# Attention scores from two matmuls in place of three: key parts stacked on the rows of the array

## The chip, the cores and the metric

The kernel runs on one core of a Trainium2 chip. The metric is the device time of one execution in microseconds (us), as the median of several runs. The profile is one execution, recorded by the hardware profiler; its times count from the start of its span.

## What is computed

The reference is a network of two layers on 512 latent tokens (x, width 1024) and 256 context tokens (ctx), in float32. Each layer normalises, projects to three head groups, mixes and projects back, then runs a gated feed-forward. The head groups are a long convolution (hyena), a gated mix over chunks of 128 tokens (sgu) and differential attention. Only the attention is touched by the change:

```python
def diff_attn_block(q, k, v, lam):
    s = jnp.einsum('bqhcd,bkhcd->bhcqk', q, k).astype(jnp.float32) * (DA_HEAD_DIM ** -0.5)
    a = jax.nn.softmax(s, axis=-1)
    w = a[:, :, 0] - lam * a[:, :, 1]
    return jnp.einsum('bhqk,bkhd->bqhd', w.astype(v.dtype), v)
...
        k_all = jnp.concatenate([k_c, k_l], axis=1)
        v_all = jnp.concatenate([v_c, v_l], axis=1)
        att_l = diff_attention(q_l, k_all, v_all, lam, subln_g[i], lam_init)
...
        if not last:
            att_c = diff_attention(q_c, k_c, v_c, lam, subln_g[i], lam_init)
```

There are 4 heads; each has two components c of 64 dimensions for q and k (both normalised and, for latents, rotated) and a value of 128. Latent queries see 512 + 256 keys in both layers; context queries see the 256 context keys, in the first layer alone.

## The kernel before

Every float32 operand of a matmul is kept as a high part and a low part in the type float32r: `split` (L230) writes hi = src on ScalarE and lo = src - hi on VectorE or POOL (GpSimd). A product is then three matmuls into one bank of PSUM, hi times hi, hi times lo and lo times hi: `mm3` (L245), lines L251, L252 and L253. Nearly all of TensorE's work goes through these three lines.

The tokens come in two streams, `lat` (512) and `con` (256). For each half j of the heads (two heads, h = 0 and 1), `kqv` (L616) projects k, q and v; `qk` (L538) takes the projected q or k per pair of token tiles, normalises, rotates, transposes each 128 x 128 block on TensorE (L593) and splits the result (L597). After the transpose the two components of a head lie on the rows: component 0 on rows 0 to 63, component 1 on rows 64 to 127. `kv_io` (L645) stores and loads the context's keys and values in DRAM. `attend` (L657) goes over query tiles qt of 128 and heads h; for each it computes the scores of both components c, three matmuls on 64 rows per source of keys (512 columns for latents, 256 for context), takes the maximum (L686) and the exponential (L691), combines the two components (L697), transposes the weights (L706) and multiplies with v (L718). For a latent query tile and a head that is twelve score matmuls: two components, each with three of 512 and three of 256 columns. The text calls this a unit.

The order of the work is set by Python generators: `woven` (L167) always advances the task with the smallest cost so far over its rate, where `self.cost` counts the time of matmuls as assumed by the program; `room` and `claim` hold a task back until the pools of buffers have space. UNITS (L127) gives the pools in units of 256 columns (1 KB on each partition): R for float32r operands, F for float32 work. The framework then orders each engine's instructions, so matmuls of other tasks stand between those of a unit in many places. Each engine runs its list in order. Weights are loaded by SP's queue; POOL's queue loads the tables of the convolution (L830) and the context's keys (L655).

The filter spectra of the convolution already use a product in two matmuls, the first on 128 rows, the second on 64:

```python
nc.tensor.matmul(flat(p.ap), lhsT=hid.hi[:, pos], rhs=w3[:, ch], start=True, stop=False)
nc.tensor.matmul(flat(p.ap), lhsT=hid.lo[half[0], pos], rhs=w3[half[0], ch], start=False, stop=True)
```

These are L905 and L906; L400 (16 short matmuls on 32 columns of the array for each weight tile) makes the modulation vectors.

Of the kernel before, what the change touches and what calls it, by code (L numbers as in the profile page):

```python
# [16 lines left out]
P = 128  # L17
# [11 lines left out]
HD = 64  # L29
# [3 lines left out]
CW = 256  # L33

TWO_PI = 2.0 * math.pi
SHARE = 4
# [89 lines left out]
BANKS = {"A": (0, 1, 6, 7), "H": (0, 1), "S": (2, 3, 4, 5), "W": (6, 7), "P": (6, 7)}  # L126
UNITS = {"R": 104, "RW": 24, "F": 44, "FW": 24}  # L127

# [21 lines left out]
class Net:  # L150
# [387 lines left out]
    def qk(self, st, l, c, i, rope):  # L538


        nc, nt, T = self.nc, st.nt, st.T
        w = self.win(st, l, c)
        outs = self.pairs(2, T)
        tab = self.rope[i]
# [44 lines left out]
        for t, _, sq in work:  # L589
            pt = self.ps("W", 2, 2, P)  # L590
            for h in range(2):
                for z in range(2):
                    nc.tensor.transpose(pt[:, h, z], sq[:, z, h * P:(h + 1) * P], self.ident)  # L593
            for h in range(2):
                src = pt[:, h].rearrange("p z q -> p (z q)")
                cols = slice(t * P, (t + 2) * P)
                self.split(src, *outs[h][:, cols])  # L597
            pt.free()
            sq.free()

    def vproj(self, st, l, c):
# [14 lines left out]
    def kqv(self, st, l, j, rope, q=True):  # L616

        n = st.T // 64
        st.held[j] = n * (3 if q else 2)
        yield from self.claim(st.held[j])  # L620
# [17 lines left out]
    def kv_load(self, st, j, mem):  # L638
        st.held[j] = 8
        yield from self.claim(8)  # L640
        st.k[j] = self.pairs(2, st.T)
        st.vv[j] = [Pair.one(self.r(2, 2, CW))]
        self.kv_io(st, j, mem, False)

    def kv_io(self, st, j, mem, store):  # L645

        off = 0
        for b in st.k[j] + st.vv[j]:
            sb = flat(b.whole.ap)
            dr = mem[:, j, off:off + sb.shape[1]]  # L650
            off += sb.shape[1]
            if store:
                self.nc.sync.dma_start(dr.bitcast(F32), sb.bitcast(F32))
            else:
                self.nc.gpsimd.dma_start(sb, dr)  # L655

    def attend(self, st, l, j, srcs):  # L657
# [9 lines left out]
        for qh in range(0, st.nt, 2):  # L667
# [3 lines left out]
            for h in range(2):  # L671
                q = st.q[j][h]
                ws = []
                for qt in (qh, qh + 1):
# [3 lines left out]
                    for c in range(2):  # L678
                        b = self.ps("S", nk)
                        r = slice(c * HD, (c + 1) * HD)  # L680
                        off = 0
                        for s in reversed(srcs):
                            self.mm3(b[:, off:off + s.T], [(q[r, qt * P:(qt + 1) * P], s.k[j][h][r, :])])
                            off += s.T
# [938 lines left out]
```

## Time and profile before

| | |
|---|---|
| median of 3 runs | 1915.76 us (1915.36 to 1921.28) |
| the profiled execution | 1918.05 us, span 1916.3 us |
| granted TensorE clock, mean | 0.963 |
| TensorE (PE) busy | 1797.2 us, 94% of the span |
| VectorE (DVE), ScalarE (ACT), GpSimd (POOL) busy | 1079.3, 676.9, 118.0 us |
| matmuls in the trace | 10938 |

PE's busy time is that of matmuls, which overlap in the records (each is shown until its end leaves the array); what a matmul costs is the step from its start to the next start. PEld are the loads of the stationary operand. A clock of 1.0 is 2.4 GHz, 0.5 is 1.2 GHz. L12 is line 12 of the kernel; for the three matmuls of `mm3` all products share the three lines, and the score matmuls are those with 64 rows.

### The profile page before, as it was taken

The numbers are of one execution on the slowest core, as the hardware profiler recorded it, in microseconds if no ns is written. First come the engines' busy times: TensorE is split into PE (matmuls) and PEld (weight loads), VectorE is DVE, ScalarE is ACT, GpSimd is POOL, SyncE is SP. The second block draws the span as 40 slices with busy tenths as digits, with TensorE's granted clock in tenths as the row PEclk, the third lists the DMA queues.
The fourth block names the chain that finished last, engine by engine and source line by source line (L and its number), as shares of the span: only waits on it lengthen the run. The fifth ranks groups of instructions, "written<-read, shape, count | busy, mean of one in ns | idle before, by whom it ended". The sixth has DMA issues, their size and how long they took to land.

```text
span 1916.3 us, 27513 instructions
## 1 busy us (share of the span) xinstructions
PE 1797.2 (94%) x10938; PEld 1532.3 (80%) x10938; DVE 1079.3 (56%) x2243; ACT 676.9 (35%) x1167; POOL 118.0 (6%) x127
## 2 busy tenths in 40 slices
PE   4799898888997999999999999899999999999999
PEld 1478798677776888888888888789988798888887
DVE  5677786876868533332323244779588773333333
ACT  2534434443535321212121222633455452222221
POOL 1100223311001000000000000011000000000000
PEclk9799899799997999999999999899999899999999
DMA  8667644335454434343424135453213222323321
GB/s 274 198 222 237 212 155 133 111 101 162 144 174 137 153 99 136 90 136 110 149 86 146 61 112 174 138 171 124 72 43 111 73 62 64 115 83 102 93 93 65
DMA packets 101819, 245.39 MB, mean 128 GB/s; under 512 B 9748, under 2 KB 21750, under 8 KB 101690
## 3 DMA queue, kind: packets, MB, share of 16 engines
q1 hardware_dynamic: 93450, 221.71, 36.3%
q0 software_dynamic: 8240, 21.92, 3.9%
q8 instruction: 86, 1.41, 0.3%
q14 instruction: 43, 0.35, 0.1%
HBM read 221.18 MB, written 22.41 MB: 127 GB/s over the span
## 4 chain that ended last, share of the span: by engine, by line
PE 72%; DVE 7%; ACT 2%; issue 1%; DMA 1%; POOL 0%; DVEq 0%; ACTq 0%
PE banks L251 23%; PE banks L252 22%; PE banks L253 22%; PE banks L706 1%; PE banks L400 1%; DVE tiny L686 1%; PE banks L279 1%; DMA F<-x_ctx 1%; DVE F L459 1%; DVE RW L233 0%; ACT F L506 0%; ACT F L691 0%; DVE F L1028 0%; DVE F L1189 0%; DVE F L1026 0%
## 5 line engine op out<-in xcount | busy, mean ns | idle before, releaser
L251 PE MATMUL banks<-R,RW 128*128 128x512 f32 (+1 forms) x1984 | 698.3, 353 | 8.1 <-ACT R L507 2.9
L252 PE MATMUL banks<-R,RW 128*128 128x512 f32 (+1 forms) x1984 | 695.2, 351 | 2.6 <-DVE R L510 2.6
L253 PE MATMUL banks<-R,RW 128*128 128x512 f32 (+1 forms) x1984 | 693.4, 350 | 1.7 <-DVE RW L233 1.7
L232 ACT ACTIVATE RW<-FW 128x1024 fp32r<-128x1024 f32 (+2 forms) x240 | 240.3, 1002 | 563.9 <-PE banks L252 427.5
L251 PEld LDWEIGHTS banks<-R,RW 128*128 128x128 f32 x1984 | 379.0, 191 | 66.8 <-issue 5.6
L252 PEld LDWEIGHTS banks<-R,RW 128*128 128x128 f32 x1984 | 378.8, 191 | 51.9 <-DVE R L510 3.9
L253 PEld LDWEIGHTS banks<-R,RW 128*128 128x128 f32 x1984 | 378.1, 191 | 50.1 <-DVE RW L233 2.1
L233 DVE TENSOR_TENSOR RW<-FW,RW 128x1024 fp32r<-128x1024 f32 (+2 forms) x228 | 263.1, 1154 | 243.5 <-ACT RW L232 225.7
L1189 DVE SCALAR_TENSOR_TENSOR F<-banks,mods,F 128x512 f32<-128x512 f32 (+1 forms) x192 | 116.3, 615 | 177.1 <-PE banks L253 150.6
L251 PE MATMUL banks<-R 128*128 128x256 f32 (+3 forms) x584 | 185.0, 336 | 30.7 <-ACT R L1039 12.3
L252 PE MATMUL banks<-RW,R 128*128 128x256 f32 x624 | 178.9, 287 | 2.3 <-DVE RW L233 2.2
L251 PE MATMUL banks<-RW,R 128*128 128x256 f32 x624 | 180.1, 289 | 0.8 <-ACT RW L232 0.7
L253 PE MATMUL banks<-RW,R 128*128 128x256 f32 x624 | 179.0, 287 | 0.0
L252 PE MATMUL banks<-R 128*128 128x256 f32 (+3 forms) x584 | 176.6, 316 | 0.0
L253 PE MATMUL banks<-R 128*128 128x256 f32 (+3 forms) x584 | 175.2, 312 | 1.3 <-DVE R L1041 1.3
L251 PEld LDWEIGHTS banks<-R 128*128 128x128 f32 (+1 forms) x584 | 114.8, 205 | 55.9 <-ACT R L1039 14.6
L1207 DVE TENSOR_TENSOR F<-F,banks 128x256 f32<-128x256 f32 (+1 forms) x71 | 40.0, 565 | 203.8 <-PE banks L253 189.9
L232 ACT ACTIVATE R<-F 128x512 fp32r<-128x512 f32 (+1 forms) x133 | 71.8, 550 | 222.9 <-DVE F L1207 159.8
L252 PEld LDWEIGHTS banks<-R 128*128 128x128 f32 (+1 forms) x584 | 117.5, 205 | 8.8 <-issue 3.0
L252 PEld LDWEIGHTS banks<-RW,R 128*128 128x128 f32 x624 | 120.8, 194 | 4.6 <-DVE RW L233 3.7
L251 PEld LDWEIGHTS banks<-RW,R 128*128 128x128 f32 x624 | 120.8, 194 | 3.7 <-issue 1.0
L253 PEld LDWEIGHTS banks<-RW,R 128*128 128x128 f32 x624 | 120.9, 194 | 0.7 <-issue 0.2
(158 smaller groups left out, 1681.1 us busy)
## 6 DMA issues: line engine op xcount, KB each, us to landing
FW<-in_ffn_w SPq DMA_DIRECT2D x104, 512.0 KB, 3.7
FW<-in_ada_w SPq DMA_DIRECT2D x96, 512.0 KB, 5.3
FW<-in_w_in_tm SPq DMA_DIRECT2D x50, 512.0 KB, 4.7
R<-in_tab POOLq DMA_DIRECT2D x28, 512.0 KB, 5.9
FW<-in_w_in_cm SPq DMA_DIRECT2D x24, 512.0 KB, 4.7
F<-x_ctx SPq DMA_DIRECT2D x36, 256.0 KB, 3.4
FW<-in_ffn_w SPq DMA_DIRECT2D x24, 384.0 KB, 3.1
x_ctx<-F SPq DMA_DIRECT2D x32, 256.0 KB, 2.4
```

The source lines that it names most:

```text
L232: self.nc.scalar.activation(hi, src, AF.Copy)
L233: (lo_eng or self.nc.vector).tensor_tensor(lo, src, hi.bitcast(F32), op=ALU.subtract)
L251: mm(out, lhsT=lh, rhs=rh, start=(i == 0), stop=False)
L252: mm(out, lhsT=lh, rhs=rl, start=False, stop=False)
L253: mm(out, lhsT=ll, rhs=rh, start=False, stop=(i == n - 1))
L279: nc.tensor.matmul(p1[:, t:t + 1], lhsT=sq[:, t * P:(t + 1) * P], rhs=self.ones[:, 0:1], start=True, stop=True)
L400: nc.tensor.matmul(pa[32 * j:32 * j + 32, :], lhsT=self.cv[:, k, :], rhs=ws[j // 2][:, j % 2, z], start=(k == 0), stop=(k == KT - 1), tile ...
L459: nc.vector.tensor_tensor(st.acc[:, cols], st.acc[:, cols], q.ap, op=ALU.add)
L686: nc.vector.tensor_reduce(m, b.ap, axis=AX.X, op=ALU.max)
L706: nc.tensor.transpose(p[:, i, z, :], ws[z][:, (a + i) * P:(a + i + 1) * P], self.ident)
L1189: self.nc.vector.scalar_tensor_tensor(x, p, self.mods[l][:, sec * 8 + k, st.v:st.v + 1], x, op0=ALU.mult, op1=ALU.add)
L1207: nc.vector.tensor_tensor(s.ap, s.ap, u, op=ALU.mult)
```

## The change

Keys: for each head the buffer has two slots of T columns, one for each component c. In slot c the high part lies on the component's own 64 rows and the low part on the other 64 rows. Queries: three slots; slot c has the high part on its own rows and, copied by a DMA on POOL's queue, again on the other rows; slot 2 has the low parts of both components, each on its own rows. A score is then one matmul on 128 rows (high part of q, doubled, times high and low part of k: two products in one) and one on 64 rows (low part of q times high part of k). The three products are the same as before. Each transposed block of 128 rows is split in two halves of 64 rows, since they go to different slots. Pool R has 108 units in place of 104, F has 40 in place of 44, and the cost given to the weaver for a score is two thirds of the old one.

```diff
+ROWS = [slice(0, HD), slice(HD, P)]
-UNITS = {"R": 104, "RW": 24, "F": 44, "FW": 24}
+UNITS = {"R": 108, "RW": 24, "F": 40, "FW": 24}
...
-        outs = self.pairs(2, T)
+        outs = [self.r(3 - i, T) for _ in range(2)]
...
             for h in range(2):
-                src = pt[:, h].rearrange("p z q -> p (z q)")
                 cols = slice(t * P, (t + 2) * P)
-                self.split(src, *outs[h][:, cols])
+                for z, own in enumerate(ROWS):
+                    src = pt[own, h].rearrange("p z q -> p (z q)")
+                    self.split(src, outs[h][own, z, cols], outs[h][ROWS[1 - z], z, cols] if i else outs[h][own, 2, cols])
             pt.free()
             sq.free()
+        if i == 0:
+            for h in range(2):
+                for z, own in enumerate(ROWS):
+                    nc.gpsimd.dma_start(outs[h][ROWS[1 - z], z], outs[h][own, z])
...
-        st.held[j] = n * (3 if q else 2)
+        st.held[j] = n * (7 if q else 4) // 2
...
-                        r = slice(c * HD, (c + 1) * HD)
+                        r, tq = ROWS[c], slice(qt * P, (qt + 1) * P)
                         off = 0
                         for s in reversed(srcs):
-                            self.mm3(b[:, off:off + s.T], [(q[r, qt * P:(qt + 1) * P], s.k[j][h][r, :])])
+                            k, out = s.k[j][h], b[:, off:off + s.T]
+                            nc.tensor.matmul(out, lhsT=q[:, c, tq], rhs=k[:, c], start=True, stop=False)
+                            nc.tensor.matmul(out, lhsT=q[r, 2, tq], rhs=k[r, c], start=False, stop=True)
+                            self.cost += s.T / 1200
                             off += s.T
```

In the changed program the two score matmuls are L692 (128 rows) and L693 (64 rows), the copies of q are L607, and other lines move down by 1 to 11 (L593 is L596, L706 is L717, L251 to L253 are L252 to L254, L830 is L841, L655 is L663).

The order on TensorE near the end of the latents' attention in the second layer (score matmuls read R alone). Before, one unit:

```order
L251 MATMUL banks<-R 128x512
L252 MATMUL banks<-R 128x512
L253 MATMUL banks<-R 128x512
L251 MATMUL banks<-R 128x256
L252 MATMUL banks<-R 128x256
L253 MATMUL banks<-R 128x256
L251 MATMUL banks<-R 128x512
L252 MATMUL banks<-R 128x512
L253 MATMUL banks<-R 128x512
L251 MATMUL banks<-R 128x256
L252 MATMUL banks<-R 128x256
L253 MATMUL banks<-R 128x256
```

Now:

```order
L692 MATMUL banks<-R 128x512
L693 MATMUL banks<-R 128x512
L692 MATMUL banks<-R 128x256
L693 MATMUL banks<-R 128x256
L692 MATMUL banks<-R 128x512
L693 MATMUL banks<-R 128x512
L692 MATMUL banks<-R 128x256
L693 MATMUL banks<-R 128x256
L717 MATMUL banks<-ident_100,F 128x128 x6
```

A unit has eight matmuls in place of twelve, and 128 and 64 rows alternate from each to the next, where all twelve had 64 rows.

The order on TensorE where the context's attention begins (L593 and L596 are the last transposes of q, L400 and L401 the modulation). Before:

```order
L593 MATMUL banks<-ident_100,F 128x128 x4
L400 MATMUL banks<-FW,cv_82 32x256 x4
L251 MATMUL banks<-R 128x256
L252 MATMUL banks<-R 128x256
L251 MATMUL banks<-R 128x256
L252 MATMUL banks<-R 128x256
```

Now:

```order
L596 MATMUL banks<-ident_100,F 128x128 x4
L401 MATMUL banks<-FW,cv_82 32x256 x16
L378 MATMUL banks<-ident_100,F 128x128 x2
L252 MATMUL banks<-R,RW 128x512
L253 MATMUL banks<-R,RW 128x512
L254 MATMUL banks<-R,RW 128x512
L692 MATMUL banks<-R 128x256
L693 MATMUL banks<-R 128x256
```

More of other work stands between the transposes and the first score, and the scores stand in pairs.

The order on POOL before the latents' first attention (L830 and L841 load tables, L655 and L663 the context's keys and values). Before:

```order
L830 DMA R<-in_tab 128x256 x6
L655 DMA R<-kv_73 128x512
L830 DMA R<-in_tab 128x256 x2
L655 DMA R<-kv_73 128x512
L655 DMA R<-kv_73 128x1024
L1025 TENSOR_TENSOR F<-F 128x256 x2
```

Now:

```order
L841 DMA R<-in_tab 128x256 x2
L607 DMA R<-R 64x512
L841 DMA R<-in_tab 128x256 x2
L663 DMA R<-kv_73 128x1024
L607 DMA R<-R 64x512 x3
L1036 TENSOR_TENSOR F<-F 128x256 x2
```

The four copies of q stand among loads that wait for buffers of the same pool.

## Rows read from the trace of the kernel before

**Rows 1.** The page, busy time of each engine in us (share of the span) and instructions.

```profile
PE 1797.2 (94%) x10938; PEld 1532.3 (80%) x10938; DVE 1079.3 (56%) x2243; ACT 676.9 (35%) x1167; POOL 118.0 (6%) x127
```

**Rows 2.** The stretches with score matmuls: length, busy us of each engine, clock, DMA.

```profile
125.00:215.00 90.00, 83.49 (x601) 66.76 (x600) 65.97 (x181) 40.77 (x86) 10.37 (x14) 0.96 0.72 234
345.00:435.00 90.00, 77.69 (x471) 64.18 (x472) 67.00 (x157) 44.09 (x88) 17.02 (x14) 0.86 0.35 106
...
500.00:585.00 85.00, 82.11 (x532) 61.33 (x532) 62.84 (x145) 41.84 (x84) 0.58 (x1) 1.00 0.50 163
...
1365.00:1435.00 70.00, 69.89 (x476) 61.19 (x475) 57.38 (x145) 36.41 (x68) 0.00 (x0) 0.98 0.12 37
...
1480.00:1545.00 65.00, 57.90 (x312) 50.06 (x312) 47.86 (x115) 33.71 (x64) 0.00 (x0) 0.84 0.21 65
```

**Rows 3.** Timeline, TensorE, feed-forward: start us, us, line, operands; first and last of ten.

```profile
1700.16 0.39 PE L251 MATMUL banks<-R,RW 128*128 128x512 f32 x1
...
1702.20 0.39 PE L251 MATMUL banks<-R,RW 128*128 128x512 f32 x1
```

**Rows 4.** Timeline, TensorE, a whole unit of the second layer.

```profile
1510.73 0.28 PE L252 MATMUL banks<-R,RW 128*128 128x256 f32 x1
1510.86 0.28 PE L253 MATMUL banks<-R,RW 128*128 128x256 f32 x1
1511.06 0.50 PE L251 MATMUL banks<-R 64*128 64x512 f32 x1
1511.40 0.39 PE L252 MATMUL banks<-R 64*128 64x512 f32 x1
1511.64 0.39 PE L253 MATMUL banks<-R 64*128 64x512 f32 x1
1511.64 0.50 PE L251 MATMUL banks<-R 64*128 64x512 f32 x2
...
1512.69 0.28 PE L253 MATMUL banks<-R 64*128 64x256 f32 x1
1512.90 0.33 PE L706 MATMUL banks<-ident,F 128*128 128x128 f32 x1
```

**Rows 5.** Groups by form, TensorE: the first matmul of each score triple.

```profile
L251 PE MATMUL banks<-R 64*128 64x512 f32 x64 | 33.0, 523 | 5.6 <-DVE F L798 2.8 <-ACT F L691 2.5
...
L251 PE MATMUL banks<-R 64*128 64x256 f32 x80 | 24.2, 316 | 1.6 <-DVE F L909 1.5
```

**Rows 6.** Timeline, TensorE, the filter spectra: 128 and 64 rows in turn.

```profile
185.60 0.50 PE L905 MATMUL banks<-R 128*128 128x512 f32 x1
186.03 0.50 PE L906 MATMUL banks<-R 64*128 64x512 f32 x1
186.46 0.50 PE L905 MATMUL banks<-R 128*128 128x512 f32 x1
186.90 0.50 PE L906 MATMUL banks<-R 64*128 64x512 f32 x1
```

**Rows 7.** Groups by form, VectorE and ScalarE: splits of 256 columns from PSUM.

```profile
L233 DVE TENSOR_TENSOR R<-banks,R 128x256 fp32r<-128x256 f32 x46 | 18.8, 417 | 1.4 <-ACT R L232 1.3
...
L232 ACT ACTIVATE R<-banks 128x256 fp32r<-128x256 f32 x46 | 17.2, 384 | 19.0 <-DVE R L233 11.7 <-PE banks L593 6.8 <-PE banks L984 0.5
```

**Rows 8.** DMA issues with KB and us to landing, and one issue on POOL's timeline.

```profile
kv<-R SPq DMA_DIRECT2D x8, 256.0 KB, 4.6
...
R<-in_tab POOLq DMA_DIRECT2D x14, 128.0 KB, 2.4
...
1444.37 0.53 POOL L655 DMA_DIRECT2D R<-kv  x1 [3.76 <-PE banks L253]
```

**Rows 9.** Timeline, TensorE, scores after a wait.

```profile
1515.74 0.79 PE L251 MATMUL banks<-R 64*128 64x512 f32 x1 [2.52 <-ACT F L691]
1516.33 0.62 PE L252 MATMUL banks<-R 64*128 64x512 f32 x1
```

**Rows 10.** The stretch around it, columns as in rows 2.

```profile
1514.00:1528.00 14.00, 12.03 (x46) 10.42 (x46) 11.07 (x33) 7.41 (x15) 0.00 (x0) 0.51 0.10 28
```

More of the change, by code (lines that the diff above doesn't have):

```diff
@@ L640, in kv_load @@
         yield from self.claim(8)
-        st.k[j] = self.pairs(2, st.T)
+        st.k[j] = [self.r(2, st.T) for _ in range(2)]
         st.vv[j] = [Pair.one(self.r(2, 2, CW))]
@@ L648, in kv_io @@
         for b in st.k[j] + st.vv[j]:
-            sb = flat(b.whole.ap)
+            sb = flat((b.whole if isinstance(b, Pair) else b).ap)
             dr = mem[:, j, off:off + sb.shape[1]]
```

## The prediction

> **What bounds the kernel now.** I read the page first: TensorE is busy 94% of the span, VectorE 56% and ScalarE 35%, so time is lost or won on TensorE unless a stretch waits [rows 1]. Then the table of stretches. The score matmuls stand in five stretches, together 400 us, and in these TensorE is busy 83.5 of 90, 77.7 of 90, 82.1 of 85, 69.9 of 70 and 57.9 of 65 us: it is idle for 28.9 us in all, and VectorE (some 300 us) follows well below it [rows 2]. So these stretches are bound by TensorE's order of work, with some waiting in the second and the last. "Busy" overstates the array, since matmuls overlap in the records; the rate is read from starts. Undisturbed 128-row matmuls of 512 columns start every 0.227 us (nine steps in 2.04 us) [rows 3], those of 256 columns every 0.12 us [rows 4].
>
> **What a score matmul costs now.** There are 144 triples, 64 with 512 columns and 80 with 256 [rows 5], all on 64 rows. In [rows 4] a whole unit of twelve (two components, each 3 x 512 and 3 x 256 columns) begins after a 128-row matmul. Three things are to be seen.
> - Streaming: 64-row matmuls step at 0.24 and 0.12 us, like those on 128 rows. Fewer rows buy nothing.
> - The change between 64 and 128 rows has a price on both sides. The last 256-column matmul ahead of it takes 0.20 us to the next start in place of 0.12, the first after it 0.34 in place of 0.23: 0.19 us for one change. Coming back, 1512.69 to 1512.90 is again 0.21 in place of 0.12.
> - The two components use different row halves, and they run partly side by side: a 512-column matmul of the second component starts at 1511.64 together with one of the first. The unit takes 1.84 us; its columns alone are 6 x 0.23 + 6 x 0.12 = 2.10, with the two edges 2.30. Side by side saves 0.46 us.
>
> **The pattern that the change makes stands already in the trace.** The filter spectra use a 128-row and a 64-row matmul in turn (L905, L906), the same shapes as the new pair. Their starts are 185.60, 186.03, 186.46 and 186.90: 0.43 us each where 0.227 would do [rows 6]. So one change of height costs 0.20 us, and in the new pairs every matmul has one on each side.
>
> **The change part by part.**
> 1. *Removed*: 144 matmuls, 64 x 0.23 + 80 x 0.12 = 24.3 us of TensorE.
> 2. *Changes of height*: in the order of the built programs I counted the places where the tile size of the array changes from one matmul to the next: 317 before, 425 now. The 64-row excursions rise from 103 to 160, because L692 and L693 alternate, while before six or twelve 64-row matmuls often stood together. 108 x 0.20 = +21.6 us.
> 3. *Side by side*: a 128-row matmul takes both halves, so nothing runs beside it. The old order has ten whole units of twelve and fifteen shorter runs with both halves; with half the saving for these, 10 x 0.46 + 15 x 0.23 = +8.0 us. Per unit: a whole one took 1.84 and some 0.2 outside it; the new eight are 4 x 0.23 + 4 x 0.12 + 8 x 0.20 = 3.0 us. A lone 256-column triple gains: 0.36 + 0.40 becomes 0.24 + 0.40. A rule of the Trainium skill (TensorEngine Tiling, Theoretical Speedup) gives up to twofold speed for operands of at most 64 rows; by it the old unit would take 1.05 us, this term would be some +21, and the sum 13 us higher. The trace shows 1.84, so the measured 0.46 stays.
>
>    TensorE together: -24.3 + 21.6 + 8.0 = +5.3 us. Little of it falls into idle time, which is 28.9 of 400 us [rows 2].
> 4. *Evictions of q and k*: each transposed block is now split in two row halves, 44 more ScalarE and 44 more VectorE instructions. Half the rows do not shorten an instruction whose columns stay, so 44 x 0.384 = 17 us and 44 x 0.417 = 18 us [rows 7]. Neither engine is the bound, and the projection matmuls of v and weights of other tasks hide them; uncovered they would cost up to 18 us, covered nothing. Nearest to cover: VectorE has about a quarter of these stretches free. I take +2.
> 5. *Copies of q*: 24 copies on POOL's queue, four for each of six q blocks, 128 KB for latents and 64 KB for context. Nothing before copies inside the chip's own memory. Nearest rows: a 128 KB load lands 2.4 us after issue, a 256 KB store from the same buffer in 4.6, and POOL holds 0.53 us to issue one [rows 8]. A score matmul thus follows its last q transpose by at least 0.38 (eviction) + 0.53 + 2.4 = 3.3 us, before about 1 us. The new order has over 20 us of other TensorE work there for the first heads' half of the latents (both layers), but only some 2.3 us for the context's first block (16 short ones, two transposes, three of 0.227 us) and 3.5 to 4 us for the other three (fifteen of 0.227 us in the last); ScalarE may also be late with the eviction. Four places at 1 us: +4; bounds 0 and 4 x 3.5 = 14, by the 4.6 us row.
>    On POOL the copies stand behind table and key loads that wait for buffers; the order shows them interleaved, and none of those loads waits for work that comes after the q transposes by more than 2 us of matmuls.
> 6. *Buffers and costs*: 4 units of 1 KB go from F to R, the weaver's costs fall by a third for scores. What is next to what changes in all queues; no row prices this. I put 0 with +-6.
>
> Sum: 5.3 + 2 + 4 = +11.3 us. The profiled execution took 1918.05 us, so it would be 1929; the median of the runs shown is 2.3 us lower, 1915.76, which gives **1927.0 us**.
>
> **The rivals.**
> - *Faster.* The changes of height cost less in the new pairs, or fall into waiting. Then -24.3 + 8.0 + 4 = -12 us, 1904. It decides at a price of (24.3 - 8.0 - 6) / 108 = 0.095 us per change. For it: the second stretch idles 12 us. Against it: [rows 6] has the very pattern, at twice that price. The Trainium skill (TensorEngine Tiling, Key Properties) says that a change of tiling mode, unlike a change of tile, drains the array; by that rule this rival falls, and the trace agrees in both: 0.20 us for the change, none between the two halves in [rows 4]. Chance 0.17.
> - *No difference.* The extra 5.3 us of TensorE and the copies' waits fall into idle time that is there anyway, 28.9 us, or the shuffled order gives back some: 1918. For it: TensorE's surplus is a difference of large terms. Chance 0.23.
> - *Much slower.* The copies are late: POOL, in order, waits for a table's buffer, all work behind the first score matmul stands still for 3.5 us at four places (+10 over the forecast), and TensorE's clock falls once more as it does now around 1515.74: there the engine had waited 2.52 us, and a first score matmul takes 0.59 us to the next start in place of 0.34 [rows 9]; in the 14 us around it the granted clock is 0.51, the lower level (1.2 GHz), and 12.0 us of busy time at half speed are 6 us lost [rows 10]. 1927 + 10 + 6 = 1943. It decides when copies land more than 4 us after the transposes. Chance 0.12.
> - The forecast itself, slower by 6 to 20 us: 0.48.
>
> **Numbers.** A measurement of this kernel tells about 0.3% (5.7 us) from no change. Slower is 0.48 + 0.12 = 0.60, within 0.23, faster 0.17. The range goes from half the removed price hidden (-8 us, 1908) to most of the late-copy case (+26, 1942).
>
> **What would show it.** In the new profile L692 and L693 of 512 columns should start 0.43 us apart, those of 256 columns 0.32; a whole unit should take 3.0 us. Copies should land in 2 to 5 us, and before the first L692 of an attention TensorE should wait about 1 us in four places. The page's TensorE count falls by 144. Wrong would be: pairs at 0.23 + 0.23, which is the first rival; or TensorE idle for several us on a copy, which is the third. If both are as foretold and the time still falls, it is the order of the other work that changed.

## The result and the profile after

The change is slower: 1984.88 us (median of 4 runs, 1980.69 to 1988.03) against 1915.79 us, a ratio of 1.0352 with a 95% interval of 1.0325 to 1.038, or +69 us. The forecast was 1927.0 us in a range of 1908 to 1942: right in its direction, wrong in its size, and above even the rival "much slower". The profiled execution took 1988.03 us, its span 1986.1 us at a mean clock of 0.943 (0.963 before).

The page, the row that answers to [rows 1]:

```profile
PE 1843.3 (93%) x10794; PEld 1542.5 (78%) x10794; DVE 1103.1 (56%) x2287; ACT 692.7 (35%) x1209; POOL 131.2 (7%) x151
```

144 matmuls are gone, VectorE has 44 and ScalarE 42 instructions more (44 each were foretold), POOL the 24 copies. But TensorE's busy time rose by 46 us.

TensorE's timeline of the kernel after, a whole undisturbed unit (start us, us, line, operands), against [rows 4]:

```profile
555.99 0.48 PE L692 MATMUL banks<-R 128*128 128x512 f32 x1
556.39 0.50 PE L693 MATMUL banks<-R 64*128 64x512 f32 x1
556.82 0.38 PE L692 MATMUL banks<-R 128*128 128x256 f32 x1
557.14 0.38 PE L693 MATMUL banks<-R 64*128 64x256 f32 x1
557.45 0.49 PE L692 MATMUL banks<-R 128*128 128x512 f32 x1
557.87 0.50 PE L693 MATMUL banks<-R 64*128 64x512 f32 x1
558.30 0.38 PE L692 MATMUL banks<-R 128*128 128x256 f32 x1
558.61 0.38 PE L693 MATMUL banks<-R 64*128 64x256 f32 x1
558.92 0.44 PE L717 MATMUL banks<-ident,F 128*128 128x128 f32 x2
```

The pairs step at 0.43 us (512 columns) and 0.32 us (256), the unit takes 2.93 us: the prices foretold (0.43, 0.32, 3.0).

So most of the time is elsewhere. Stretches with score matmuls, aligned between the two kernels by the same transposes and ends (length; busy us and instructions of PE, PEld, DVE, ACT, POOL; clock; DMA share; GB/s). First the kernel after:

```profile
125.00:225.00 100.00, 87.47 (x551) 64.48 (x550) 63.31 (x169) 38.55 (x80) 14.21 (x21) 0.87 0.64 203
345.00:440.00 95.00, 79.56 (x388) 61.96 (x386) 58.94 (x144) 38.33 (x79) 22.09 (x20) 0.71 0.30 89
505.00:560.00 55.00, 45.52 (x242) 36.49 (x241) 38.23 (x98) 24.91 (x53) 2.10 (x4) 0.84 0.45 125
1390.00:1440.00 50.00, 49.79 (x343) 45.10 (x343) 32.44 (x80) 25.82 (x50) 2.11 (x4) 1.00 0.32 90
1500.00:1545.00 45.00, 42.89 (x217) 31.55 (x218) 35.91 (x89) 22.08 (x44) 2.58 (x5) 1.00 0.41 124
```

The same stretches of the kernel before:

```profile
125.00:208.00 83.00, 78.78 (x580) 63.05 (x579) 59.59 (x164) 37.18 (x77) 8.35 (x12) 0.98 0.70 227
320.00:406.00 86.00, 70.89 (x454) 59.15 (x453) 64.48 (x157) 40.52 (x83) 19.93 (x18) 0.88 0.32 97
475.00:514.00 39.00, 36.21 (x250) 30.95 (x249) 34.04 (x92) 21.98 (x46) 0.63 (x1) 1.00 0.51 163
1334.00:1384.00 50.00, 49.82 (x353) 45.96 (x352) 28.79 (x73) 23.41 (x43) 0.00 (x0) 1.00 0.25 79
1442.00:1475.00 33.00, 32.95 (x198) 26.32 (x196) 29.07 (x71) 18.65 (x37) 0.53 (x1) 1.00 0.40 131
```

The five are 17, 9, 16, 0 and 12 us longer. They don't hold quite the same work: outside the scores the second has 38 matmuls fewer than before and the fifth 35 more, some 7.5 us of its 12, so these lengths are rough. In the third (223 and 224 other matmuls) and the fourth (328 and 327) the work is the same. Where the copies had over 20 us of other TensorE work ahead and the work is the same (the fourth), nothing is lost; the second stretch also had that cover, and its scores wait for no copy, so its loss has another cause. In the first three TensorE is idle for 12.5, 15.4 and 9.5 us (before 4.2, 15.1 and 2.8) and its clock is lower. By the page, 2 x (1 - clock) x span, the time at the lower level, is 226 us, 142 before.

TensorE's timeline of the kernel after, the start of the third attention block:

```profile
539.52 0.39 PE L254 MATMUL banks<-R,RW 128*128 128x512 f32 x1
543.54 0.50 PE L692 MATMUL banks<-R 128*128 128x512 f32 x1 [3.63 <-DMA R<-R]
543.97 0.79 PE L693 MATMUL banks<-R 64*128 64x512 f32 x1
544.70 0.58 PE L692 MATMUL banks<-R 128*128 128x256 f32 x1
...
553.04 0.63 PE L254 MATMUL banks<-R,RW 128*128 128x512 f32 x1
553.47 0.63 PE L252 MATMUL banks<-R,RW 128*128 128x512 f32 x1
553.89 0.53 PE L253 MATMUL banks<-R,RW 128*128 128x512 f32 x1
554.26 0.39 PE L254 MATMUL banks<-R,RW 128*128 128x512 f32 x1
```

TensorE waits 3.63 us for a copy of q. It is the longest of the waits that the profile puts down to the copies (us in all, times, longest):

```profile
PE banks L692 <- DMA R<-R: 6.3, 3, 3.6
```

A further wait of 2.09 us, ahead of the score that starts at 197.13, ends where a copy lands (197.00), though the profile names another releaser. The copies are thus waited for some 8 us in all. Right after the longest wait the pair steps at 0.73 us and ordinary matmuls at 0.43 us, until 553.9. The table of stretches has that piece, columns as above:

```profile
543.60:553.90 10.30, 10.30 (x22) 6.47 (x23) 4.17 (x8) 2.17 (x4) 0.00 (x0) 0.52 0.34 66
```

A clock of 0.52 (the level of 1.2 GHz) for 10.3 us of full work costs another 5 us: a late copy is paid more than once.

The copies wait for something themselves. POOL's timeline of the kernel after, the four copies of that block:

```profile
536.95 0.55 POOL L607 DMA_DIRECT2D R<-R  x1 [32.67 <-ACT R L233]
538.78 0.53 POOL L607 DMA_DIRECT2D R<-R  x1 [1.28 <-ACT R L233]
539.98 0.51 POOL L607 DMA_DIRECT2D R<-R  x1 [0.67 <-ACT R L233]
541.87 0.51 POOL L607 DMA_DIRECT2D R<-R  x1 [1.38 <-ACT R L233]
```

The first copy is issued 1.0 us after the start of the last transpose (535.97), the fourth 5.9 us after it; POOL waits for ScalarE's evictions of q, not for loads. The DMA of the stretch from 536 to 545 us (tenths of the 16 engines' busy time in 40 slices; then the copies' issues, KB each, median us to landing):

```profile
DMA  0000099199953889999879999999989999999998
...
R<-R POOLq DMA_DIRECT2D x4, 128.0 KB, 6.5
```

The DMA engines are busy with weights, an input and the copies themselves, and the copies take 6.5 us to land: 536.95 + 6.5 is 543.45, and the score starts at 543.54. Over the whole span the row that answers to [rows 8] is:

```profile
R<-R POOLq DMA_DIRECT2D x16, 128.0 KB, 4.2
...
R<-R POOLq DMA_DIRECT2D x8, 64.0 KB, 6.0
```

ScalarE's timeline of the kernel after says why the later evictions come late, here in the second layer:

```profile
1519.98 0.78 ACT L233 ACTIVATE R<-banks 64x256 fp32r<-64x256 f32 x2 [0.70 <-DVE R L234]
1521.54 0.38 ACT L233 ACTIVATE R<-banks 64x256 fp32r<-64x256 f32 x1 [0.78 <-DVE R L234]
1522.82 0.85 ACT L233 ACTIVATE RW<-FW 128x768 fp32r<-128x768 f32 x1 [0.90 <-PE banks L253]
1523.69 0.38 ACT L233 ACTIVATE R<-banks 64x256 fp32r<-64x256 f32 x1
1525.02 0.38 ACT L233 ACTIVATE R<-banks 64x256 fp32r<-64x256 f32 x1 [0.95 <-DVE R L234]
```

Before three of these five evictions of q (the line of RW is another's) ScalarE waits for VectorE's subtraction of an earlier half, though the halves are different rows of the bank.

From the trace's starts, over the score matmuls and over all matmuls (a step is from a start to the next start, without idle time, and with time at the lower clock counted by half; us; the kernels e1 to e13 are those of the experiments):

| kernel | scores: steps | idle ahead | lost by lower clock | all: steps | idle ahead | lost by lower clock |
|---|---|---|---|---|---|---|
| before | 79.9 | 7.2 | 6.1 | 1738.9 | 114.6 | 58.0 |
| after | 96.2 | 18.6 | 17.5 | 1750.5 | 138.4 | 92.4 |
| e1, copies by ScalarE | 97.0 | 11.3 | 11.1 | 1754.3 | 130.7 | 72.7 |
| e2, grouped by height | 76.4 | 19.9 | 13.2 | 1727.7 | 142.0 | 86.9 |
| e3, three on own rows | 79.0 | 10.5 | 10.0 | 1738.4 | 128.0 | 67.1 |
| e10, e3 staged, no copies | 79.1 | 11.0 | 10.2 | 1737.0 | 123.5 | 67.6 |
| e12, rows in turn | 67.8 | 6.6 | 5.3 | 1726.2 | 123.7 | 55.0 |
| e13, lower cost alone | 78.2 | 13.8 | 8.5 | 1737.1 | 123.4 | 71.0 |

At the scores the change thus loses 16 us in steps and 23 in waiting and clock, 39 of its 69 us. The other 30 lie in other matmuls. Over all matmuls it is 12 us of work at full clock, 24 of waiting and 34 of lower clock: in these executions **half of the loss is the clock, not the work**. The table is of one execution of each kernel, and the mean clock of a kernel's executions differs by up to 0.013 (e5, 0.955 to 0.968), where 0.01 is some 19 us; so its columns of waiting and clock are rough.

### The profile page after: what moved, and what is told of

It reads as the page before. It is cut to its first block, busy times and chain, and to the rows that moved or that the text cites. A ratio compares the mean times of both kernels' runs of the same rounds, so it can differ in the third digit from the quotient of the medians.

```text
span 1986.1 us, 27404 instructions
## 1 busy us (share of the span) xinstructions
PE 1843.3 (93%) x10794; PEld 1542.5 (78%) x10794; DVE 1103.1 (56%) x2287; ACT 692.7 (35%) x1209; POOL 131.2 (7%) x151
## 4 chain that ended last, share of the span: by engine, by line
PE 64%; DVE 7%; issue 3%; ACT 2%; DMA 1%; POOL 0%; DVEq 0%; ACTq 0%; POOLq 0%
PE banks L252 19%; PE banks L253 19%; PE banks L254 19%; PE banks L693 2%; PE banks L692 2%; DVE R L234 1%; PE banks L401 1%; DVE RW L234 1%; PE banks L717 1%; ACT F L507 0%; PE banks L280 0%; DVE F L1200 0%; DVE F L460 0%; DVE F L1039 0%; PE banks L294 0%
## 5 line engine op out<-in xcount | busy, mean ns | idle before, releaser
L252 PE MATMUL banks<-R,RW 128*128 128x512 f32 (+1 forms) x1984 | 700.3, 354 | 10.9 <-ACT R L508 4.1
L253 PE MATMUL banks<-R,RW 128*128 128x512 f32 (+1 forms) x1984 | 696.9, 352 | 0.5 <-DVE R L511 0.3
L254 PE MATMUL banks<-R,RW 128*128 128x512 f32 (+1 forms) x1984 | 694.4, 350 | 0.2 <-DVE RW L234 0.2
L252 PEld LDWEIGHTS banks<-R,RW 128*128 128x128 f32 x1984 | 379.2, 192 | 70.0 <-issue 7.3
L233 ACT ACTIVATE RW<-FW 128x1024 fp32r<-128x1024 f32 (+2 forms) x240 | 240.2, 1001 | 543.1 <-PE banks L253 403.8
L253 PEld LDWEIGHTS banks<-R,RW 128*128 128x128 f32 x1984 | 379.4, 191 | 49.2 <-DVE R L511 1.6
L254 PEld LDWEIGHTS banks<-R,RW 128*128 128x128 f32 x1984 | 379.1, 191 | 48.8 <-issue 0.6
L253 PE MATMUL banks<-RW,R 128*128 128x256 f32 x624 | 180.8, 290 | 2.2 <-DVE RW L234 2.2
L252 PE MATMUL banks<-RW,R 128*128 128x256 f32 x624 | 180.5, 290 | 1.3 <-DVE F L1200 1.2
L254 PE MATMUL banks<-RW,R 128*128 128x256 f32 x624 | 179.6, 288 | 0.0
L252 PE MATMUL banks<-R 128*128 128x256 f32 (+1 forms) x440 | 137.4, 323 | 29.2 <-ACT R L1050 17.8
L233 ACT ACTIVATE R<-F 128x512 fp32r<-128x512 f32 (+1 forms) x133 | 72.2, 549 | 235.3 <-DVE F L1218 153.2
L253 PE MATMUL banks<-R 128*128 128x256 f32 (+1 forms) x440 | 136.1, 313 | 0.8 <-DVE R L234 0.5
L254 PE MATMUL banks<-R 128*128 128x256 f32 (+1 forms) x440 | 133.3, 308 | 1.6 <-DVE R L1052 1.6
L253 PEld LDWEIGHTS banks<-RW,R 128*128 128x128 f32 x624 | 121.5, 195 | 5.4 <-DVE RW L234 3.3
L252 PEld LDWEIGHTS banks<-R 128*128 128x128 f32 x440 | 94.6, 220 | 38.1 <-ACT R L1050 20.2
L252 PEld LDWEIGHTS banks<-RW,R 128*128 128x128 f32 x624 | 121.4, 195 | 3.4 <-DVE F L1200 1.4
L254 PEld LDWEIGHTS banks<-RW,R 128*128 128x128 f32 x624 | 121.6, 195 | 1.0 <-issue 0.2
L702 ACT ACTIVATE F<-banks,tiny,rq 128x768 f32<-128x768 f32 (+1 forms) x80 | 72.3, 906 | 82.0 <-DVE tiny L700 57.9
```

Source lines behind the costliest of these rows:

```text
L233: self.nc.scalar.activation(hi, src, AF.Copy)
L252: mm(out, lhsT=lh, rhs=rh, start=(i == 0), stop=False)
L253: mm(out, lhsT=lh, rhs=rl, start=False, stop=False)
L254: mm(out, lhsT=ll, rhs=rh, start=False, stop=(i == n - 1))
L702: nc.scalar.activation(es[c].ap, b.ap, AF.Exp, bias=m, scale=scale, accum_out=sums[c])
```

## The experiments

All are timed in three rounds against the kernel before on the same chip; a ratio is to that, with its 95% interval. The kernel before itself took 1916 to 1920 us on the different chips, so kernels of different chips are compared by their ratios (0.01 is 19 us). Since the weaver and the framework may shuffle everything else when one thing changes, I also compared the sequence of the 10506 matmuls outside the scores in the traces (line, operands and shape) and counted the fewest that have to move to make one sequence of the other. **After against before it is 744.** A pair of kernels with few moved tells of its edit; one with many tells of edit and order together.

### Copies, halves, heights

**e1**, the change with the DMA copies replaced by ScalarE writing the high part a second time:

```diff
+                    if i == 0:
+                        nc.scalar.activation(outs[h][ROWS[1 - z], z, cols], src, AF.Copy)
...
-                    nc.gpsimd.dma_start(outs[h][ROWS[1 - z], z], outs[h][own, z])
```

> The change, with the doubled high part of q written by a second ScalarE instruction from PSUM in place of the DMA copy; everything else stays. Theory COPIES (scores wait for the landing of the copies, and the clock falls behind these waits): most of the 69 us go, about 1945, and TensorE waits for no DMA ahead of a score. Theory HALVES (splitting each transposed block in row halves makes a longer chain between ScalarE and VectorE, which read one bank of PSUM in turn, and the scores wait for its end): 40 more ScalarE instructions lengthen the chain, so 1985 or more. Theory HEIGHTS (the alternation of 128 and 64 rows, beyond its 0.2 us a change, keeps the clock low): about 1975, the waits alone gone. Theory ORDER (pool sizes and costs shuffle the other work): near 1985.

Measured 1963.74 us, 1.0231 (1.0207 to 1.0256): **21 us less than the change**, 23 by the ratios; 95 matmuls moved against it. By the table the work at full clock grows by 4 us, the waiting falls by 8 and the loss by the lower clock by 20; by the mean clock of all four executions of each (0.945 and 0.951) it is 12. The third stretch in the kernel e1, again from the transposes to some 16 scores, and TensorE's timeline of its last transposes and first scores:

```profile
488.00:535.00 47.00, 41.88 (x247) 34.59 (x246) 38.91 (x101) 28.54 (x62) 0.00 (x0) 0.93 0.41 135
...
518.14 0.60 PE L596 MATMUL banks<-ident,F 128*128 128x128 f32 x4
...
519.51 0.39 PE L690 MATMUL banks<-R 128*128 128x512 f32 x1
519.83 0.49 PE L691 MATMUL banks<-R 64*128 64x512 f32 x1
```

The first score starts 1.4 us after the start of the last four transposes and waits for nothing; in the change it is 7.9 us (535.64 to 543.54). The stretch takes 47 us in place of 55, 39 before: half of its loss is gone. 5 us of idle time and a clock of 0.93 are left.

**e2**, the change with, per component, both 128-row matmuls and then both 64-row ones:

```diff
+                        for k, out in parts:
+                            nc.tensor.matmul(out, lhsT=q[:, c, tq], rhs=k[:, c], start=True, stop=False)
+                        for k, out in parts:
+                            nc.tensor.matmul(out, lhsT=q[r, 2, tq], rhs=k[r, c], start=False, stop=True)
```

> The change, with the matmuls of a component grouped: both 128-row matmuls first, then both 64-row ones, so a latent unit has four changes of height in place of eight. COPIES and HALVES: about 64 x 2 x 0.2 = 26 us of TensorE less at most, some of it hidden, 1965 or more, and the waits stay. HEIGHTS: the clock recovers too, 1945 or less. ORDER: between 1960 and 1985.

Measured 1961.44 us, 1.0209 (1.0189 to 1.0229): **23 us less**, 27 by the ratios, with 9 matmuls moved. The trace has 315 places where the array's tile size changes instead of 425; 110 x 0.20 = 22 us. By the table, steps fall by 20 us at the scores and by 23 over all matmuls, so the price of a change of height is confirmed; the wait for copies stays.

**e3**, the change with three 64-row matmuls on the component's own rows; copies issued, but unread:

```diff
-                            nc.tensor.matmul(out, lhsT=q[:, c, tq], rhs=k[:, c], start=True, stop=False)
-                            nc.tensor.matmul(out, lhsT=q[r, 2, tq], rhs=k[r, c], start=False, stop=True)
+                            nc.tensor.matmul(out, lhsT=q[r, c, tq], rhs=k[r, 0], start=True, stop=False)
+                            nc.tensor.matmul(out, lhsT=q[r, c, tq], rhs=k[r, 1], start=False, stop=False)
+                            nc.tensor.matmul(out, lhsT=q[r, 2, tq], rhs=k[r, 0], start=False, stop=True)
```

> The change with the scores again from three matmuls of 64 rows on the component's own rows; the halved evictions, the three slots of q, the pool sizes and the copies by DMA stay, but no matmul reads what the copies write. COPIES or HEIGHTS: near the kernel before, 1915 to 1930. HALVES: most of the loss stays, 1950 or more. ORDER: most of the loss stays too, 1950 or more.

Measured 1940.61 us, 1.0103 (1.0088 to 1.0118), 260 moved against the change: 44 us less than the change, 48 by the ratios. That is near the sum of e1 and e2 (23 + 27), but e2 took out only part of the alternation, so the sum proves nothing: e3 also has the 144 matmuls again, 152 changes of height fewer than e1 (273 against 425), and is 25 us faster than e1. Still 20 above before.

**e4**, the kernel before with evictions in row halves:

```diff
-                self.split(src, *outs[h][:, cols])
+                hi, lo = outs[h].ap
+                for own in (slice(0, HD), slice(HD, P)):
+                    src = pt[own, h].rearrange("p z q -> p (z q)")
+                    self.split(src, hi[own, cols], lo[own, cols])
```

> The kernel before, with nothing changed but the eviction of the transposed blocks: each is split in two row halves, as in the change. HALVES: 1940 or more. COPIES, HEIGHTS and ORDER: within 10 us of the kernel before.

Measured 1942.45 us, 1.01 (1.0066 to 1.0133), with 154 moved: the halves alone cost some 20 us in the kernel before.

### Why the halves cost: number or turns

**e5**, the kernel before with halves, but first the whole block copied from PSUM to SBUF by one ScalarE instruction; the halves are split from there. **e6**, the change with the same staging.

```diff
+            sb = self.f(2, 2 * P)
+            nc.scalar.activation(sb.ap, pt.ap.rearrange("p h z q -> p h (z q)"), AF.Copy)
+            pt.free()
...
+                    self.split(sb[own, h], hi[own, cols], lo[own, cols])
```

> The kernel before with halved evictions, as in the run of the halves alone (about 22 us slower than before), but the whole transposed block is first copied to SBUF by one ScalarE instruction, and the halves are split from there. Theory TURNS (ScalarE and VectorE take turns at one PSUM bank, so eight instructions of a block follow one another and hold its bank): the loss goes, 1915 to 1928. Theory COUNT (88 more instructions on two engines cost time wherever they read): 22 more ScalarE instructions of about 0.6 us make it 1942 or more.

> The change with the whole block copied to SBUF first and the halves split from there; the DMA copies and the alternation of heights stay. TURNS: about 20 us less than the change, 1965. COUNT: 1985 or more. If the waits for the copies dominate instead, nothing is gained, since the copies still start after the last split.

e5: 1918.49 us, 0.9999 (0.9984 to 1.0014), 144 moved. More instructions than e4, and the loss is gone, so it isn't their number. What is gone with it is the two engines' reading from the bank in turns; that the bank also comes free earlier was not tested apart. Groups by form, ScalarE (busy us, mean ns | idle us before them, by what), in the kernel e4:

```profile
L232 ACT ACTIVATE R<-banks 64x256 fp32r<-64x256 f32 x88 | 32.9, 376 | 34.3 <-DVE R L233 25.6 <-PE banks L593 7.9
```

and in the kernel e5:

```profile
L232 ACT ACTIVATE R<-F 64x256 fp32r<-64x256 f32 x88 | 36.5, 415 | 1.9
```

25.6 us of waiting for VectorE, 11.7 in [rows 7], go to nothing when the source is no PSUM bank. How they reach TensorE the traces don't show: its idle time ahead of scores is lower in e4 than before (5.4 against 7.2 us).

e6: 1976.9 us, 1.0301 (1.0276 to 1.0326), 174 moved: 8 us less than the change, 10 by the ratios, half of what was expected. It doesn't take the halves' delay out by itself: the staged evictions let the first copy of a block go out 1.7 to 7.8 us after the start of its last transpose, 1.0 to 1.8 in the change, and TensorE's wait for copies in e6 grows from 6.3 us:

```profile
PE banks L695 <- DMA R<-R: 9.9, 4, 4.2
```

### All three taken away, and 19 us left

**e7**: ScalarE doubles, grouped by whole unit (four 128-row matmuls, then four of 64 rows). **e8**: staged, POOL doubles from SBUF, grouped by unit (the line on POOL is e8's; e7 has that of e1).

```diff
-                    nc.gpsimd.dma_start(outs[h][ROWS[1 - z], z], outs[h][own, z])
...
+                        nc.gpsimd.tensor_copy(outs[h][ROWS[1 - z], z, cols], src)
...
+                    for c, k, out in parts:
+                        nc.tensor.matmul(out, lhsT=q[:, c, tq], rhs=k[:, c], start=True, stop=False)
+                    for c, k, out in parts:
+                        nc.tensor.matmul(out, lhsT=q[r, 2, tq], rhs=k[r, c], start=False, stop=True)
```

> The change with the doubled part of q written by ScalarE (no copies by DMA) and the matmuls of a whole unit grouped: four of 128 rows, then four of 64 rows, two changes of height in place of eight. If the three causes add up (copies 21 us, heights 24 us for grouping by component and a few more by unit, halves 20 us): 1935 or a little less. If they overlap (a lost stretch at the lower clock counted twice): 1945 or more.

> The change with all three causes taken away: whole blocks copied to SBUF before the halves, the doubled part of q written by GpSimd (POOL) from there in place of the DMA, matmuls grouped by unit. If the causes add up and TURNS holds: 1905 to 1922, at or below the kernel before, since 24 us of TensorE streaming are gone. COUNT: 1935 or more.

e7 1939.44 us, 1.0104 (1.0084 to 1.0124); e8 1937.83 us, 1.0098 (1.0072 to 1.0124). Both keep about 20 us.

**e9**, the kernel before with R 108 and F 40 alone; **e10**, e3 with staged evictions and without copies; **e11**, e8 grouped by component as in e2. The edit of e9 (those of e10 and e11 are pieced together from the diffs above):

```diff
-UNITS = {"R": 104, "RW": 24, "F": 44, "FW": 24}
+UNITS = {"R": 108, "RW": 24, "F": 40, "FW": 24}
```

> The kernel before with the pools of the change alone (R 108, F 40). Open is what is left when the copies, the bank's turns and most changes of height are gone: that kernel (staged evictions, doubling by POOL, grouped by unit) still took 1937.8 us, 19 above the kernel before, though its TensorE work at full clock is some 11 us less. POOLS: four units of F fewer hold tasks back, so this kernel takes 1928 to 1940 us. Theories LATENCY (grouping by unit lets the first component's maximum and exponential start later) and FORM (doubling and splitting of q make the chain from transposes to the first score longer): the pools cost nothing, 1913 to 1922 us.

> The change with staged evictions and three 64-row matmuls on a component's own rows, so no doubled queries and no copies; pools, slots and the weaver's costs for scores as in the change. POOLS: 1928 to 1940 us, as slow as the pools alone, and the three matmuls are innocent. LATENCY and FORM: nothing of what they blame is in it, 1915 to 1923 us, like the kernel before with staged evictions (1918.5).

> Staged evictions, doubling by POOL from the staged block, no DMA copies, as in the kernel of 1937.8 us, but grouped by component (both 128-row matmuls, then both 64-row ones) in place of by unit. Twice as many changes of height in each unit: two round trips instead of one, 0.4 us for each of 36 units, so +8 to +15 us of TensorE by the heights alone, 1946 to 1952. LATENCY: the first component's maximum starts some 1.4 us earlier in a unit, which gives back the heights' cost and more, 1925 to 1940 us. FORM and POOLS: heights alone decide, 1946 to 1952.

e9 1915.39 us, 0.9988 (0.9976 to 1.0): the pools are innocent, though 631 matmuls moved. e10 1937.56 us, 1.0109 (1.0089 to 1.0129): **three old matmuls, no copies and no turns on a bank are still 21 us slower**, so a loss of this size needs neither FORM nor LATENCY. e11 1940.61 us, 1.0123 (1.0098 to 1.0147), 5 us above e8 by the ratios. Its trace has 310 changes of height and e8's 290, so the heights cost only 20 x 0.20 = 4 us, not the 8 to 15 expected, and nothing is left for LATENCY to give back. In e10, 702 matmuls have moved against the kernel before. What it has left of the change is the pools, the third slot and the cost, and the order that these make: by the table some 9 us more of waiting and 10 of lower clock, with no more work.

**e13**, the kernel before with a score's cost for the weaver cut by a third; **e14**, before with the change's pools and a third, unused slot of q, claimed. **e15** and **e16**: e8 and the change with the old cost. One line or two for each:

```diff
                             self.mm3(b[:, off:off + s.T], [(q[r, qt * P:(qt + 1) * P], s.k[j][h][r, :])])
+                            self.cost -= s.T / 2400
```

```diff
-        outs = self.pairs(2, T)
+        outs = [Pair.one(self.r(3 - i, T)) for _ in range(2)]
...
-        st.held[j] = n * (3 if q else 2)
+        st.held[j] = n * (7 if q else 4) // 2
```

```diff
-                            self.cost += s.T / 1200
+                            self.cost += s.T / 800
```

> The kernel before, with the weaver's cost of a score cut by a third as in the change; matmuls, pools and evictions untouched. The kernel with staged evictions and three own-row matmuls took 1937.6 us, 19 more than staged evictions alone, and the pools alone cost nothing. What is left in it of the change is the score's cost and the third slot of q. COST (the weaver lets the attention run too early against the projections, so that first scores and exponentials are waited for): 1930 to 1940 us. SLOT (half a q buffer more is claimed, so k, q and v are let in later): 1913 to 1921 us.

> The kernel before with the pools of the change, and with q buffers of three slots of which two are used, claimed as in the change; the score's cost as before. SLOT: 1930 to 1940 us. COST: 1912 to 1920 us. Both in part: between, and the two together make the 19.

> Staged evictions, doubling by POOL, grouped by unit (1937.8 us), with the weaver's cost of a score as before the change. COST: the 19 us go, and TensorE's work, 11 us less than before, is left: 1908 to 1922 us. SLOT: 1933 to 1942 us, unchanged.

> The change with nothing else than the weaver's cost of a score as before. COST: 15 to 20 us less than the change, 1963 to 1972 us. SLOT: 1980 to 1990 us. A third way: with the scores set later against other work, the copies gain cover, and more than 20 us go, below 1963.

e13 1936.17 us, 1.0086 (1.0056 to 1.0116), 519 moved: **a number that costs no engine anything is worth 17 us.** e14 1923.49 us, 1.0023 (1.0001 to 1.0044): some 4, hardly clear of nothing. e15 1932.72 us, 1.0082 (1.0058 to 1.0106), and e16 1974.9 us, 1.0291 (1.0251 to 1.0332): by the ratios 3 us less than e8, within the noise, and 12 less than the change, not the 17.

**e17**, the cost raised by a third in the kernel before (`+=` in that line of e13).

> The kernel before with the weaver's cost of a score a third higher in place of a third lower (which cost 17 us). DIRECTION (a lower cost lets the attention run too early, so its matmuls wait for exponentials): a higher one does no harm, 1910 to 1921 us. SCATTER (any other cost makes another order, and the one before was a lucky one): 1925 to 1940 us.

e17 1946.4 us, 1.0152 (1.012 to 1.0183), 556 moved: **29 us slower**, so DIRECTION falls. Neither a lower nor a higher cost is the good one. But not every other order is worse, as SCATTER has it: e9 has more matmuls moved than either and loses nothing. Why the old cost gives a good order is not shown. TensorE's longest waits, in e13 (us in all, times, longest):

```profile
PE banks L400 <- DMA FW<-in_ada_w: 23.0, 10, 9.6
PE banks L251 <- ACT F L692: 14.7, 8, 3.2
```

and in e17:

```profile
PE banks L400 <- DMA FW<-in_ada_w: 26.1, 11, 9.1
PE banks L279 <- DVE F L459: 13.6, 4, 9.3
```

Each order has its own waits: exponentials (L692, L691 before) in e13, where the kernel before has 6.3 us, the normalisation's sums (L279) in e17, where it has 4.4 us.

### A version that beats both

**e12**, the kernel before with the two components' matmuls in turn, so that neighbours use different row halves and different banks; **e18**, the same with the cost up by a third.

```diff
+                        for i, (x, y) in enumerate(((qh_, kh_), (qh_, kl_), (ql_, kh_))):
+                            for c in range(2):
+                                r = slice(c * HD, (c + 1) * HD)
+                                nc.tensor.matmul(bs[c][:, off:off + s.T], lhsT=x[r, tq], rhs=y[r, :], start=i == 0, stop=i == 2)
+                        self.cost += 6 * s.T / 2400
```

> A version that may beat both: the kernel before, its three 64-row matmuls per score and its evictions untouched, but the two components' matmuls in turn, so that neighbours use different halves of the array's rows and write different banks. In the kernel before only the seam between the components ran side by side (a unit of 1.84 us where its columns and two edges are 2.30). SIDE BY SIDE: every pair runs together, the unit takes 1.05 + 0.4 = 1.3 to 1.5 us, 36 units of 0.3 to 0.5 us are 11 to 18 us of TensorE; 1900 to 1910 us. If the change between halves costs something as the change of height does: 11 of them in each unit at 0.2 us, +80 us, 1990. LATENCY: the first component's maximum starts later, the gain is given back, 1912 to 1930.

> The two components' matmuls in turn (1910.6 us, the fastest so far) with the weaver's cost of a score a third higher. DIRECTION: 1903 to 1912 us. SCATTER: 1915 to 1930 us.

e12 1910.56 us, 0.9967 (0.9956 to 0.9978), 137 moved: 6 us below the kernel before and the fastest here, though short of the 1900 to 1910 expected. TensorE's timeline of e12, a whole unit (x12, one line):

```profile
1497.35 0.39 PE L253 MATMUL banks<-R,RW 128*128 128x512 f32 x1
1497.66 1.53 PE L686 MATMUL banks<-R 64*128 64x512 f32 x12
1499.12 0.39 PE L251 MATMUL banks<-R,RW 128*128 128x256 f32 x1
```

1.46 us to the next start, where [rows 4] has 1.84. Of the 16 whole units in e12, without idle time, five take 1.24 to 1.31 us and five others 1.87 to 2.2; before, six of ten take 1.83. By the table TensorE's work falls by 13 us, 12 of them at the scores, the loss by the lower clock by 3, and 9 us more of waiting in other matmuls take most of it back. e18 1943.12 us, 1.0145 (1.0109 to 1.018): its order gives back five times the gain.

## Why the prediction was wrong

Two steps of the prediction failed. Part 5 priced a late copy by TensorE's wait alone and put the lower clock after it at nothing; part 6 put the order at 0 +-6. Measured are 21 to 23 us for the copies, of which some 8 are waiting and 12 to 20 the clock (e1), and 21 us for what e10 keeps of the change, which is the order with the third slot.

The account that the runs support, by the ratios: from before to e10 21 us, the order with the third slot (4 alone, e14); from e10 to e3, the halves, nothing clear of noise; from e3 to e1 25 us, two matmuls that alternate in place of three; from e1 to the change 23 us, the copies. Each of these holds waiting and lower clock elsewhere, too, as the table has it. How the first 21 divide stays open: the cost alone is worth 17 in the kernel before, but the old cost gives back 12 in the change (e16) and next to nothing in e8 (e15), and e10 with the old cost was not run.

- **Parts 1 to 3, TensorE** (-24.3 + 21.6 + 8.0 = +5.3): the prices are right. 144 matmuls are gone, pairs step at 0.43 and 0.32 us, a unit takes 2.93 us, the trace has 425 changes, and 110 fewer of them gave some 23 us (e2). The sum is too small: over all matmuls the work at full clock rises by 11.6 us. The difference of large terms hid that the alternation alone is worth 22 us, which grouping avoids. In nearly one order (e3 to e1) the replacement adds 152 changes, not 108, and costs 25 us: 16 of work, the rest waiting and lower clock.
- **Part 4, evictions** (+2, bounds 0 to 18): the bound was made by busy time, "covered nothing". Wrong in kind: the cost is not 44 more instructions on each engine (e5 has more) but goes with the turns on one bank. Alone some 20 us (e4), above the upper bound; in the change's order 0 to 10 (e10 to e3, e6). A trace of it stood in [rows 7]: 11.7 us of ScalarE's idle time "<-DVE R L233".
- **Part 5, copies** (+4, bounds 0 to 14): measured 21 to 23 (e1). Its "a 128 KB load lands 2.4 us after issue" was too low for them: the copies took 4.2 us, and 6.5 in the third block. But the waits that came of it, some 8 us, lie within the bounds. The step that failed is that the wait was the whole price: 12 to 20 us are the lower clock, which was put into a rival alone, once, though [rows 9, 10] price it for any place with a wait. This is the rival "much slower", with its threshold of 4 us met at three of the four places (the first copy lands 5.3, 6.5, 7.5 and 3.7 us after the start of the last transpose). Its reason, POOL held by a table's buffer, was not what happened: POOL waited for ScalarE. "ScalarE may also be late with the eviction" was right for the later copies of a block; how the delay divides between eviction and landing e6 doesn't tell, since its first copies go out later.
- **Part 6, order** (0 +-6): the largest miss in kind. Both halves of "buffers and costs" were one line; the pools were worth nothing (e9), the cost 17 us alone (e13), and 29 us the other way (e17). The trace gave no price for it, so the bound of 6 us was chosen, not worked out. The built programs would have shown how much of the order moves, but not its price: e9 moves as many matmuls and costs nothing.
- **The rivals.** "Faster" had its point at 0.095 us per change: the change costs 0.20, so it fell as argued. The direction was right for reasons that were given, more work on TensorE and waits for copies, but these as priced make 11 of the 69 us. The Trainium skill (TensorEngine Tiling (Array Packing), Theoretical Speedup) gives up to twofold speed for operands of at most 64 rows; 1.84 us for a unit was set against it. The trace of e12 goes further towards that rule: the order within a unit decides, and units of 1.24 us, where the columns alone are 2.10, were reached.

## What to carry to other kernels

Where a scheduler sets the order by costs, changing a cost is an edit of its own: build the edit with the old cost first, and time the cost alone, in both directions, before any gain or loss is put down to the instructions. Price an eviction by its chain (who else reads that bank, and who waits for the last piece), not by busy time; and a wait on TensorE by its length and the lower clock after it: here the clock cost more than the waits for the copies. Where two matmuls use different row halves, try them next to each other before stacking operands: that needs no copy and no new layout, and here gave 6 us.

## What was not expected of the hardware

- ScalarE's reads of one half of the rows of a PSUM bank often waited for VectorE's reads of the other half: 25.6 us of ScalarE's waiting in e4, 1.9 us of any idle time when the same 88 splits read SBUF (e5). Whether the chip or the framework's semaphores demand it was not tried.
- A copy inside SBUF by POOL's queue took 4.2 us for 128 KB (6.5 in the third block, where the DMA engines were busy throughout) and 6.0 us for 64 KB to land. The smaller were not the faster, but all eight of them fell into the first stretch, where the DMA engines were busiest (a share of 0.64).
- After a wait of 3.63 us TensorE's granted clock was 0.52 for 10.3 us of full work, some 5 us on top of the wait.
- Two 64-row matmuls on different row halves, issued in turn into different banks, brought a unit of 2.10 us of columns down to 1.24 us at best (e12).
